# Taking the two heads on the two partition halves together in the mixer's attention, their products issued alternately

## The chip, the cores and the metric

The kernel runs on one core of one Trainium2 chip. The metric is the time of one execution on the device in microseconds (us). Three runs of the kernel before took 1867.41 to 1868.89 us, median 1867.45.

## What is computed

Two residual blocks over 512 positions of width 1024, all in float32: a Conformer-like block (SwiGLU feed-forward, a mixer, SwiGLU feed-forward) and a block with an mLSTM and an RG-LRU layer. The change lies in the mixer, between its input projection and its output projection. Cut to that, the reference is:

```python
u = rms_norm(h, mix_norm)
qa, ka, va, qb, kb, vb, ga, gb = jnp.split(u @ w_in, SPLITS, axis=-1)
ya = neighbourhood_attention_2d(qa, ka, va, na_rpb)   # 8 heads of 64, 8 rows x 16 columns around a query
yb = windowed_gqa_sink(rope(qb), rope(kb), vb, sink)  # 8 query heads of 64 on 2 kv heads, |i-j| <= 128
merged = sigmoid(ga) * (ya @ w_branch_a) + sigmoid(gb) * (yb @ w_branch_b)
h = h + merged @ w_out
```

Both attentions are a score product, a softmax and a value product. In the first a bias is added to the scores; in the second a sink logit joins the denominator.

## The kernel before, in words

**Layout.** Activations lie with features on the 128 partitions and the 512 positions along the free axis. A head is 64 wide, so a tile of queries or keys holds two heads: one on partitions 0 to 63, one on 64 to 127. All projections are one function, `group` (L143): per 128 rows of input three matmuls of 512 columns (`mm3`, L111 to L114; float32 is cut in a high and a low part). A projection with eight input tiles takes 24 such matmuls, and so do the two groups of a `branch` (L310). The attention's own products take float32 operands directly; each such matmul shows in the trace as two passes, each with a weight load, while a transpose shows as one.

**Neighbourhood attention** runs over 16 iterations (L462): tile i (four of them), half hf of the query blocks (two), head e (two).
- `na_scores` (L332) contracts over the 64 partitions of one head: for hf = 0 two matmuls of 256 columns (L343), for hf = 1 one of these and two with 64x64 weights (L346, L347) that go to partitions 0 to 63 and 64 to 127 of the same PSUM tile. `softmax` (L318) adds the bias and takes the row extreme on VectorE (L320), then the exponential and its sum on ScalarE (L322); VectorE scales by the reciprocal (L357, L360).
- `na_values` (L363) transposes the probabilities in pieces of 128 columns on TensorE (L368), copies them to SBUF on ScalarE (L370), and multiplies 64 columns of values by them (L376, L379, L380). The output goes to the head's 64 partitions of the accumulator `po`.

**Windowed attention** runs over 8 iterations (L474): query block nb (four), key-value head g (two).
- `gqa_scores` (L396) makes four matmuls on the 64 partitions of head g (L405), 256 columns wide for nb = 0 and 3, 384 for nb = 1 and 2, each with its softmax, then the scaling (L411 to L416).
- `gqa_values` (L419) goes over two or three key blocks: four transposes (L426), one copy of 512 columns (L428), one product of 512 columns (L429) into half of `po`. `gqa_out` (L432) writes the result (L438, L439) to `yb`.

**Order of the work.** Both loops are pipelined by hand: the scores of the next iteration stand ahead of the values of this one, and in between stands `fills` (L457), which takes projections from a list of 26 (four for later q and k tiles, six for the second attention's inputs, eight gates, the four branches of the first attention, four more gates). In the first loop one fill stands in each iteration, in the second one or two. Behind the loops follow four gates (L486) and the branches of the second attention. The tile framework then orders the instructions of each engine: the earliest in the program goes first if its inputs and its output tile are there, otherwise a later one passes it. The trace shows this order as it came out.

**Tiles.** PSUM has two pools of four banks: `bank` (projections) and `cbank` (scores, transposes, `po`). The pool `chain` (L54) has 18 SBUF tiles: biases, mask, probabilities, the shifted scores `sx`, the transposed copies, and the eight tiles `ya` of the first attention's result, which the four branches of the fill list read.

Of the kernel before, what the change touches and what calls it, by code (L numbers as in the profile page):

```python
# [14 lines left out]
P = 128  # L15
# [7 lines left out]
BIG = 3e38  # L23
# [19 lines left out]
def kernel(ctx: ExitStack, tc: tile.TileContext, a, out):  # L43
# [184 lines left out]
    def mixer(x):  # L228
# [103 lines left out]
        def na_scores(i, hf, e):  # L332
            bias_tile(i)
            if hf:
                bias_tile(4 + i // 2)
            ro = slice(64 * e, 64 * e + 64)
            wid = (256, 256) if hf == 0 else (256, 128)
            ps = cbank()
            for j in range(2):
                b = 2 * hf + j  # L340
                pj = ps[:, 256 * j : 256 * j + wid[j]]
                if b < 3:
                    PE.matmul(pj, qc[i][ro, 64 + 128 * b : 192 + 128 * b], kc[i][ro, 128 * b : 128 * b + 256],  # L343
                              start=True, stop=True)
                else:
                    PE.matmul(pj[0:64], qc[i][ro, 0:64], kc[i][ro, 0:128], start=True, stop=True)  # L346
                    PE.matmul(pj[64:128], qc[i][ro, 448:512], kc[i][ro, 384:512], start=True, stop=True)  # L347
            nm, sm, rc = small(2), small(2), small(2)
            pm = ctile()
            for j in range(2):  # L350
                if 2 * hf + j < 3:
                    bt = bias[i][:, e * 256 : e * 256 + 256]
                else:
                    bt = bias[4 + i // 2][:, (2 * (i % 2) + e) * 128 : (2 * (i % 2) + e) * 128 + 128]
                c = slice(256 * j, 256 * j + wid[j])
                softmax(ps[:, c], wid[j], pm[:, c], bt, nm, sm, j, BIG)
            V.reciprocal(rc, sm)  # L357
            for j in range(2):
                c = slice(256 * j, 256 * j + wid[j])
                V.tensor_scalar(pm[:, c], pm[:, c], rc[:, j : j + 1], None, op0=ALU.mult)  # L360
            return pm, sum(wid)

        def na_values(i, hf, e, po, pm, tot):  # L363
            ro = slice(64 * e, 64 * e + 64)
            hd = slice((2 * i + e) * 64, (2 * i + e) * 64 + 64)
            pt = cbank()
            for c in range(0, tot, P):
                PE.transpose(pt[:, c : c + P], pm[:, c : c + P], ident)  # L368
            ptc = ctile()
            S.copy(ptc[:, :tot], pt[:, :tot])  # L370
            for j in range(2):
                b = 2 * hf + j
                if b < 3:
                    for kb in range(2):
                        c = 256 * j + kb * P
                        PE.matmul(po[ro, 64 + 128 * b : 192 + 128 * b], va[b + kb][:, hd], ptc[:, c : c + P],  # L376
                                  start=kb == 0, stop=kb == 1)
                else:
                    PE.matmul(po[ro, 0:64], va[0][:, hd], ptc[:, 256:320], start=True, stop=True)  # L379
                    PE.matmul(po[ro, 448:512], va[3][:, hd], ptc[:, 320:384], start=True, stop=True)  # L380
# [15 lines left out]
        def gqa_scores(nb, g):  # L396
# [3 lines left out]
            ro = slice(64 * g, 64 * g + 64)  # L400
            nm, sm = small(4), small(4)
            es = []
            for i in range(4):
                ps = cbank()
                PE.matmul(ps[:, :n], bq[i][ro, nb * P : nb * P + P], bk[0][ro, b0 * P : b1 * P], start=True, stop=True)  # L405
                e = ctile()
                softmax(ps[:, :n], n, e[:, :n], mask[0][:, mo : mo + n], nm, sm, i,
                        nsink[0][:, 4 * g + i : 4 * g + i + 1])
                es.append(e)
            rc = small(4)  # L410
            V.tensor_tensor(rc, nm, vc("sink", 4 * g, 4), op=ALU.add)  # L411
            S.activation(rc, rc, AF.Exp)
            V.tensor_tensor(rc, rc, sm, op=ALU.add)
            V.reciprocal(rc, rc)
            for i in range(4):
                V.tensor_scalar(es[i][:, :n], es[i][:, :n], rc[:, i : i + 1], None, op0=ALU.mult)  # L416
            return es

        def gqa_values(nb, g, po, es):  # L419
            b0, b1 = max(0, nb - 1), min(4, nb + 2)  # L420
            ro = slice(64 * g, 64 * g + 64)
            for kb in range(b0, b1):
                pt = cbank()
                for i in range(4):
                    c = (kb - b0) * P
                    PE.transpose(pt[:, i * P : (i + 1) * P], es[i][:, c : c + P], ident)  # L426
                ptc = ctile()
                S.copy(ptc, pt)  # L428
                PE.matmul(po[ro, :], bv[0][:, kb * P + 64 * g : kb * P + 64 * g + 64], ptc,  # L429
                          start=kb == b0, stop=kb == b1 - 1)  # L430
# [31 lines left out]
        its = [(i, hf, e) for i in range(4) for hf in range(2) for e in range(2)]  # L462
        sc = na_scores(*its[0])
        for n, it in enumerate(its):
            fills()
            nxt = na_scores(*its[n + 1]) if n + 1 < len(its) else None
            if n % 4 == 0:
                po = cbank()
            na_values(*it, po, *sc)
            if n % 4 == 3:  # L470
# [573 lines left out]
```

## Time and profile before

| | |
|---|---|
| median of three runs | 1867.45 us |
| the profiled execution, its own time | 1867.34 us |
| its span in the trace | 1865.6 us |
| mean granted TensorE clock | 0.998 |
| TensorE matmul busy (PE) | 1842.9 us, 99% |
| TensorE weight load busy (PEld) | 1488.2 us, 80% |
| VectorE (DVE) / ScalarE (ACT) / GpSimd (POOL) busy | 1085.9 / 709.4 / 23.9 us |
| the stretches of the two attentions | 422.4 to 555.1 us, 555.1 to 666.0 us |

The span is what the trace covers; 1.7 us of the execution lie outside it. Matmul times in the trace overlap (a matmul starts before the one ahead has ended), so the cost of a matmul is read from the distance of two starts, not from its duration. In the timeline one row can stand for several matmuls; its time is from the first start to the last end.

### The profile page before, as it was taken

Reading aid. Unit: us, or ns where it says so; the run is one execution under the profiler, and the core shown is the slowest. Engines: PE = TensorE matmul, PEld = TensorE weight load, DVE = VectorE, ACT = ScalarE, POOL = GpSimd, SP = SyncE. Lnnn points to the kernel's source line nnn. Section 1 sums busy time; section 2 is a strip of 40 time slices with the busy share of each in tenths; the row PEclk is TensorE's granted clock in tenths of the full one; section 3 lists DMA queues with packets and bytes.
Section 4 is the critical chain, followed back from the end, with each engine's and each line's share of the span. In section 5 each row is a group of like instructions: output and inputs, shape, how many; then the busy total and the mean of one; then the engine's idle time right before and its main releaser. Section 6 shows DMA issues by size and latency. Waiting matters only on the chain.

```text
span 1865.6 us, 21147 instructions
## 1 busy us (share of the span) xinstructions
PE 1842.9 (99%) x8320; PEld 1488.2 (80%) x8320; DVE 1085.9 (58%) x1728; ACT 709.4 (38%) x1050; POOL 23.9 (1%) x53
## 2 busy tenths in 40 slices
PE   8999999999999999999999999999999999999998
PEld 6888888877776678788888888788887888888886
DVE  5634435734645456453543475867467476798785
ACT  4322213423344444231322252433434334446762
POOL 0000000000000000000000000000000000000000
PEclk9999999999999999999999999999999999999999
DMA  5332322322321122232232232223222222323222
GB/s 192 93 102 91 102 95 86 102 96 95 103 73 46 57 80 91 90 102 94 99 101 91 85 108 90 80 74 102 74 91 91 79 91 68 101 88 98 88 68 79
DMA packets 50018, 169.53 MB, mean 91 GB/s; under 512 B 5760, under 2 KB 5888, under 8 KB 49920
## 3 DMA queue, kind: packets, MB, share of 16 engines
q1 hardware_dynamic: 48048, 164.91, 26.9%
q10 hardware_dynamic: 1872, 3.29, 0.5%
q8 instruction: 65, 1.06, 0.2%
q14 instruction: 33, 0.27, 0.0%
HBM read 164.77 MB, written 2.10 MB: 89 GB/s over the span
## 4 chain that ended last, share of the span: by engine, by line
PE 85%; issue 12%; DVE 1%; ACT 1%; POOL 1%; DMA 0%; POOLq 0%; ACTq 0%
PE bank L114 25%; PE bank L112 25%; PE bank L113 25%; PE cbank L429 1%; PE cbank L405 1%; PE cbank L662 1%; PE cbank L112 1%; PE cbank L113 1%; PE cbank L114 1%; PE cbank L343 1%; PE cbank L376 1%; POOL small L178 1%; PE cbank L685 1%; PE cbank L686 1%; PE cbank L426 1%
## 5 line engine op out<-in xcount | busy, mean ns | idle before, releaser
L112 PE MATMUL bank<-act,hi 128*128 128x512 f32 x1944 | 760.4, 392 | 6.8 <-ACT act L138 6.7
L113 PE MATMUL bank<-act,hi 128*128 128x512 f32 x1944 | 760.6, 391 | 1.0 <-DVE act L123 0.5
L114 PE MATMUL bank<-act,lo 128*128 128x512 f32 x1944 | 759.7, 391 | 0.0
L97 ACT CAST hi<-raw 128x1024 fp32r<-128x1024 f32 (+2 forms) x315 | 323.2, 1027 | 837.2 <-PE bank L113 541.6
L99 DVE TENSOR_TENSOR lo<-raw,hi 128x1024 fp32r<-128x1024 f32 (+2 forms) x315 | 375.3, 1192 | 135.7 <-ACT hi L97 135.2
L112 PEld LDWEIGHTS bank<-act,hi 128*128 128x128 f32 x1944 | 365.4, 188 | 86.8 <-ACT act L138 6.7
L113 PEld LDWEIGHTS bank<-act,hi 128*128 128x128 f32 x1944 | 365.5, 188 | 84.0 <-DVE act L123 3.8
L114 PEld LDWEIGHTS bank<-act,lo 128*128 128x128 f32 x1944 | 365.6, 188 | 78.2 <-issue 3.1
L196 DVE TENSOR_TENSOR act<-bank,rb 128x512 f32<-128x512 f32 x70 | 48.3, 690 | 117.5 <-PE bank L114 117.3
L223 DVE SCALAR_TENSOR_TENSOR h<-bank,h 128x512 f32<-128x512 f32 x48 | 33.2, 692 | 112.2 <-PE bank L114 111.9
L112 PE MATMUL bank<-hi,act 128*128 128x512 f32 x224 | 88.5, 395 | 0.0
L114 PE MATMUL bank<-hi,act 128*128 128x512 f32 x224 | 87.9, 393 | 0.0
L216 DVE TENSOR_TENSOR act<-bank,rb 128x512 f32<-128x512 f32 x42 | 29.0, 691 | 101.1 <-PE bank L114 101.1
L113 PE MATMUL bank<-lo,act 128*128 128x512 f32 x224 | 87.8, 392 | 0.0
L121 ACT CAST act<-act 128x512 fp32r<-128x512 f32 x96 | 59.6, 621 | 69.4 <-DVE act L217 28.7
L123 DVE TENSOR_TENSOR act<-act 128x512 fp32r<-128x512 f32 x96 | 65.9, 686 | 12.9 <-ACT act L121 12.2
L785 DVE SCALAR_TENSOR_TENSOR act<-act,vec 128x511 f32<-128x511 f32 (+2 forms) x84 | 62.7, 747 | 1.7
L112 PE MATMUL bank<-chain,hi 128*128 128x512 f32 x160 | 62.6, 392 | 0.0
L113 PE MATMUL bank<-chain,hi 128*128 128x512 f32 x160 | 62.6, 391 | 0.0
L114 PE MATMUL bank<-chain,lo 128*128 128x512 f32 x160 | 62.5, 391 | 0.0
L198 ACT ACTIVATE act<-act 128x512 f32<-128x512 f32 x72 | 45.3, 630 | 31.1 <-DVE act L196 30.7
L200 DVE SCALAR_TENSOR_TENSOR act<-act 128x512 f32<-128x512 f32 x72 | 49.4, 686 | 8.7 <-ACT act L198 8.7
(225 smaller groups left out, 1614.2 us busy)
## 6 DMA issues: line engine op xcount, KB each, us to landing
raw<-in_gu_dram SPq DMA_DIRECT2D x88, 512.0 KB, 3.2
raw<-in_mh_dram SPq DMA_DIRECT2D x64, 512.0 KB, 3.2
raw<-in_win_dram SPq DMA_DIRECT2D x34, 512.0 KB, 3.2
raw<-in_dn_dram SPq DMA_DIRECT2D x32, 512.0 KB, 3.5
raw<-in_mo_dram SPq DMA_DIRECT2D x16, 512.0 KB, 3.2
raw<-in_dn_dram SPq DMA_DIRECT2D x16, 384.0 KB, 3.1
raw<-in_rxr_dram SPq DMA_DIRECT2D x12, 512.0 KB, 3.2
raw<-in_rg_dram SPq DMA_DIRECT2D x12, 512.0 KB, 3.2
```

The source lines that it names most:

```text
L97: S.copy(hi[:, :cols], raw[:, :cols])
L99: V.tensor_tensor(lo[:, :cols], raw[:, :cols], f(hi[:, :cols]), op=ALU.subtract)
L112: PE.matmul(ps, st[0], mv[0], start=start, stop=False)
L113: PE.matmul(ps, st[0], mv[1], start=False, stop=False)
L114: PE.matmul(ps, st[1], mv[0], start=False, stop=stop)
L121: S.copy(hi, x)
L123: V.tensor_tensor(lo, x, f(hi), op=ALU.subtract)
L196: V.tensor_tensor(g, ps, rb, op=ALU.mult)
L198: S.activation(th, g, AF.Tanh, scale=0.5)
L200: V.scalar_tensor_tensor(s, th, 1.0, g, op0=ALU.add, op1=ALU.mult)
L223: V.scalar_tensor_tensor(x[o], ps, 0.25, x[o], op0=ALU.mult, op1=ALU.add)
L785: V.scalar_tensor_tensor(c[:, s:], t[:, : T - s], vc(w, j * nt + i), c[:, s:], op0=ALU.mult, op1=ALU.add)
```

## The change

In both attentions one iteration now handles both heads of a tile. The first loop has 8 iterations (i, hf), the second 4 (nb).
- Scores: two `cbank` tiles, one for each head; the matmuls of the heads alternate.
- Values: both heads are transposed and copied first (the second head's transposes go to a tile of the pool `bank`), then the value products alternate, head by head, into the two halves of `po`.
- Fills: in the first loop one before and one after the next scores; in the second one within the scores, after the second pair, one before and one after them (none within or ahead of those of nb = 0 but the one within). The list itself and the pools stay as they are.

The softmax, scaling and output lines are the same instructions for each head, in the order first head, second head.

```diff
@@ na_scores
+            pss = [cbank() for _ in range(2)]
+            ros = [slice(64 * e, 64 * e + 64) for e in range(2)]
             for j in range(2):
                 b = 2 * hf + j
+                for e, ro in enumerate(ros):
+                    pj = pss[e][:, 256 * j : 256 * j + wid[j]]
+                    if b < 3:
+                        PE.matmul(pj, qc[i][ro, 64 + 128 * b : 192 + 128 * b], kc[i][ro, 128 * b : 128 * b + 256],
+                                  start=True, stop=True)
+                    else:
+                        PE.matmul(pj[0:64], qc[i][ro, 0:64], kc[i][ro, 0:128], start=True, stop=True)
+                        PE.matmul(pj[64:128], qc[i][ro, 448:512], kc[i][ro, 384:512], start=True, stop=True)
...
@@ na_values
+            for e, pm in enumerate(pms):
+                pt = (cbank, bank)[e]()
...
+                S.copy(ptc[:, :tot], pt[:, :tot])
+                ptcs.append(ptc)
             for j in range(2):
                 b = 2 * hf + j
+                for kb in range(2):
+                    for e, ptc in enumerate(ptcs):
...
+                            PE.matmul(po[ro, 64 + 128 * b : 192 + 128 * b], va[b + kb][:, hd], ptc[:, c : c + P],
+                                      start=kb == 0, stop=kb == 1)
...
@@ gqa_scores
             for i in range(4):
+                pss = [cbank() for _ in range(2)]
+                for ps, ro in zip(pss, ros):
+                    PE.matmul(ps[:, :n], bq[i][ro, nb * P : nb * P + P], bk[0][ro, b0 * P : b1 * P],
+                              start=True, stop=True)
...
+                if i == 1:
+                    fills(1)
...
@@ gqa_values
             for kb in range(b0, b1):
+                ptcs = []
+                for g in range(2):
+                    pt = (cbank, bank)[g]()
...
+                    S.copy(ptc, pt)
+                    ptcs.append(ptc)
+                for g, ptc in enumerate(ptcs):
+                    PE.matmul(po[64 * g : 64 * g + 64, :], bv[0][:, kb * P + 64 * g : kb * P + 64 * g + 64], ptc,
+                              start=kb == b0, stop=kb == b1 - 1)
...
@@ the loops
-        its = [(i, hf, e) for i in range(4) for hf in range(2) for e in range(2)]
+        its = [(i, hf) for i in range(4) for hf in range(2)]
...
             fills()
             nxt = na_scores(*its[n + 1]) if n + 1 < len(its) else None
+            fills()
...
+        sc = gqa_scores(0, fills)
+        for nb in range(4):
+            fills()
+            nxt = gqa_scores(nb + 1, fills) if nb < 3 else None
+            fills()
+            po = cbank()
+            gqa_values(nb, po, sc)
+            gqa_out(nb, po)
             sc = nxt
```

## Rows read from the trace of the kernel before

**Rows 1.** The page, part 1: busy time of the engines and share of the span.

```profile
PE 1842.9 (99%) x8320; PEld 1488.2 (80%) x8320; DVE 1085.9 (58%) x1728; ACT 709.4 (38%) x1050; POOL 23.9 (1%) x53
```

**Rows 2.** Busy time by stretch: time, then each engine, granted clock, DMA share, GB/s.

```profile
422.40:555.10 132.70, 132.70 (x658) 98.34 (x657) 67.35 (x163) 47.97 (x108) 0.96 (x3) 1.00 0.27 88
555.10:666.00 110.90, 110.82 (x445) 69.89 (x443) 56.54 (x157) 49.12 (x121) 0.00 (x0) 1.00 0.16 53
```

**Rows 3.** Timeline of TensorE, one score block between projections: start, time, what, count.

```profile
428.63 0.39 PE L113 MATMUL bank<-act,hi 128*128 128x512 f32 x1
428.85 0.39 PE L114 MATMUL bank<-act,lo 128*128 128x512 f32 x1
429.17 1.13 PE L343 MATMUL cbank<-act 64*128 64x256 f32 x4
430.23 0.66 PE L368 MATMUL cbank<-ident,chain 128*128 128x128 f32 x4
430.64 0.48 PE L112 MATMUL bank<-act,hi 128*128 128x512 f32 x1
430.96 0.39 PE L113 MATMUL bank<-act,hi 128*128 128x512 f32 x1
```

**Rows 4.** Timeline, a score block with the 64x64 products, weight loads (PEld) too.

```profile
437.53 0.70 PE L343 MATMUL cbank<-act 64*128 64x256 f32 x2
...
438.16 0.32 PE L346 MATMUL cbank<-act 64*64 64x128 f32 x1
...
438.16 0.32 PE L347 MATMUL cbank<-act 64*64 64x128 f32 x1
...
438.21 0.13 PEld L346 LDWEIGHTS cbank<-act 64*64 64x64 f32 x1
...
438.32 0.27 PE L347 MATMUL cbank<-act 64*64 64x128 f32 x1
...
438.52 0.66 PE L368 MATMUL cbank<-ident,chain 128*128 128x128 f32 x4
```

**Rows 5.** Groups by line, 422.3 to 666: busy us, mean ns of one.

```profile
L343 PE MATMUL cbank<-act 64*128 64x256 f32 x48 | 14.6, 411 | 0.0
L376 PE MATMUL cbank<-chain,v 128*64 128x128 f32 x96 | 13.9, 281 | 0.0
L405 PE MATMUL cbank<-act 64*128 64x384 f32 x32 | 11.4, 495 | 0.0
L405 PE MATMUL cbank<-act 64*128 64x256 f32 x32 | 8.5, 396 | 0.0
L343 PEld LDWEIGHTS cbank<-act 64*128 64x128 f32 x48 | 7.7, 185 | 6.1 <-PE bank L113 3.9 <-issue 1.4 <-DVE act L280 0.4
```

**Rows 6.** Timeline of TensorE, windowed attention: two blocks of scores.

```profile
590.23 2.84 PE L405 MATMUL cbank<-act 64*128 64x384 f32 x8
...
640.64 1.99 PE L405 MATMUL cbank<-act 64*128 64x256 f32 x8
```

**Rows 7.** Timeline of TensorE, first attention: a block of value products.

```profile
440.96 1.09 PE L376 MATMUL cbank<-chain,v 128*64 128x128 f32 x8
```

**Rows 8.** Timeline, windowed attention: three copies (ACT) and the value products behind them.

```profile
614.00 1.52 ACT L428 COPY chain<-cbank 128x512 f32<-128x512 f32 x3
...
614.90 1.07 PE L429 MATMUL cbank<-chain,act 128*64 128x512 f32 x2
615.90 0.50 PE L114 MATMUL bank<-act,lo 128*128 128x512 f32 x1
616.24 0.40 PE L112 MATMUL bank<-act,hi 128*128 128x512 f32 x1
616.57 1.07 PE L429 MATMUL cbank<-chain,act 128*64 128x512 f32 x2
```

**Rows 9.** Groups by line, 555 to 666: the softmax of the windowed attention, ScalarE and VectorE.

```profile
L322 ACT ACTIVATE chain<-chain,small 128x384 f32<-128x384 f32 x16 | 9.8, 612 | 6.1 <-DVE small L320 6.1
L320 DVE CUSTOM_DVE_ANT_0 chain<-cbank,chain,nsink 128x384 f32<-128x384 f32 x16 | 9.4, 617 | 0.7 <-PE cbank L405 0.5 <-ACT chain L322 0.2
```

More of the change, by code (lines that the diff above doesn't have):

```diff
@@ L348, in na_scores @@
[L348 to L360, printed above, removed]
@@ new lines, in na_scores @@
+            pms = []
+            for e, ps in enumerate(pss):
+                nm, sm, rc = small(2), small(2), small(2)
+                pm = ctile()
+                for j in range(2):
+                    if 2 * hf + j < 3:
+                        bt = bias[i][:, e * 256 : e * 256 + 256]
+                    else:
+                        bt = bias[4 + i // 2][:, (2 * (i % 2) + e) * 128 : (2 * (i % 2) + e) * 128 + 128]
+                    c = slice(256 * j, 256 * j + wid[j])
+                    softmax(ps[:, c], wid[j], pm[:, c], bt, nm, sm, j, BIG)
+                V.reciprocal(rc, sm)
+                for j in range(2):
+                    c = slice(256 * j, 256 * j + wid[j])
+                    V.tensor_scalar(pm[:, c], pm[:, c], rc[:, j : j + 1], None, op0=ALU.mult)
+                pms.append(pm)
@@ L394, in gqa_consts, with gqa_scores @@
             nsink.append(t)
-        def gqa_scores(nb, g):
+        def gqa_scores(nb, fills):
             b0, b1 = max(0, nb - 1), min(4, nb + 2)
@@ L399, in gqa_scores @@
             mo = (b0 - nb + 1) * P
-            ro = slice(64 * g, 64 * g + 64)
-            nm, sm = small(4), small(4)
-            es = []
+            ros = [slice(64 * g, 64 * g + 64) for g in range(2)]
+            nms, sms = ([small(4) for _ in range(2)] for _ in range(2))
+            es = ([], [])
             for i in range(4):
[L404 to L409, printed above, removed]
@@ new lines, in gqa_scores @@
+                for g, ps in enumerate(pss):
+                    e = ctile()
+                    softmax(ps[:, :n], n, e[:, :n], mask[0][:, mo : mo + n], nms[g], sms[g], i,
+                            nsink[0][:, 4 * g + i : 4 * g + i + 1])
+                    es[g].append(e)
+                if i == 1:
+                    fills(1)
+            for g in range(2):
+                rc = small(4)
+                V.tensor_tensor(rc, nms[g], vc("sink", 4 * g, 4), op=ALU.add)
+                S.activation(rc, rc, AF.Exp)
+                V.tensor_tensor(rc, rc, sms[g], op=ALU.add)
+                V.reciprocal(rc, rc)
+                for i in range(4):
+                    V.tensor_scalar(es[g][i][:, :n], es[g][i][:, :n], rc[:, i : i + 1], None, op0=ALU.mult)
@@ L417, in gqa_scores, with gqa_values @@
             return es
-        def gqa_values(nb, g, po, es):
+        def gqa_values(nb, po, es):
             b0, b1 = max(0, nb - 1), min(4, nb + 2)
-            ro = slice(64 * g, 64 * g + 64)
             for kb in range(b0, b1):
[L423 to L430, printed above, removed]
+                ptcs = []
+                for g in range(2):
+                    pt = (cbank, bank)[g]()
+                    for i in range(4):
+                        c = (kb - b0) * P
+                        PE.transpose(pt[:, i * P : (i + 1) * P], es[g][i][:, c : c + P], ident)
+                    ptc = ctile()
+                    S.copy(ptc, pt)
[3 more added lines that the diff above has]
+                              start=kb == b0, stop=kb == b1 - 1)
```

62 lines of the change are left out of this document (16 added, 46 removed).

## The prediction, made before the changed kernel was run

> **What bounds the kernel now.** I read the page first: TensorE is busy for 99% of the span, the next engine for 58% [rows 1]. A gain must therefore be TensorE time; time taken from VectorE or ScalarE buys nothing unless TensorE waits for it. Then the windows of the two attentions: 132.7 and 110.9 us, TensorE busy throughout at a granted clock of 1.00, which is its 2.4 GHz level, while VectorE has 67 and 57 us of work and ScalarE 48 and 49 [rows 2]. So TensorE bounds both stretches, and about half of the other engines' time is free.
>
> Next the timeline of TensorE, for what a block of attention products costs there. Projections start 0.22 us apart. The last one before a score block is followed after 0.32, and the first one behind the transposes is followed after 0.32 as well [rows 3]: going into a block with narrower weights and coming back costs about 0.10 each way, 0.2 a block. The score block itself, two matmuls in four passes on one half of the partitions, holds TensorE for 1.06 us (429.17 to 430.23) [rows 3]. With the mean duration of one pass, 0.411 [rows 5], the distance of two passes is (1.13 - 0.41) / 3 = 0.24 us; the rest of the 1.06 is the tail until other weights follow. In the windowed attention a pass takes (2.84 - 0.495) / 7 = 0.335 us at 384 columns and (1.99 - 0.396) / 7 = 0.228 at 256 [rows 5, 6].
>
> The row that decides is one where two products use different parts of the array. L346 and L347 have 64x64 weights on the same partitions and write to the two partition halves of one PSUM tile. Their first passes start together at 438.16, their second ones at 438.32 [rows 4]: four passes, two at a time. Side by side is thus possible here, for float32 operands with two passes each. A pair of passes took 0.16 us; one pass of the same 128 columns alone takes (1.09 - 0.281) / 7 = 0.116 [rows 5, 7]. The pair was 1.38 times as long as one, where one behind the other would be 2 times.
>
> **The change part by part.** The sum is made against the profiled execution, 1867.34 us; the median of the runs is 0.1 above it, so nothing is corrected.
>
> *Scores of the first attention.* Before, each of 8 (tile, half) pairs has two blocks; after, one. All inputs are there, the two PSUM tiles are free, and so the order should keep the heads alternating. The heads lie on different halves of the partitions and write to different banks. A pair-step lies between 1.0 and 1.38 times a single step if they overlap. The 0.16 us of the pair in the trace are above its 0.13 us weight load [rows 4], so there the load seems to set the pace; here the load takes 0.185 and the step is already 0.24 [rows 5]. I take 1.0. Then a block for both heads takes what one head's took, and per tile one block of 1.06 [rows 3] and one of 438.52 - 437.53 = 0.99 [rows 4] go away: 4 x 2.05 = **-8.2 us**. Bounds: at 1.38, 8 blocks x 3 steps x 0.24 x 0.38 = 2.2 of this comes back; if the second head's 64x64 pair runs behind the first's, 4 x 0.32 = 1.3. Eight ways in are saved, but the transposes, which followed the scores directly, now come behind a fill, so eight ways out are added: 0.
>
> *Scores of the windowed attention.* Before, 8 blocks of 8 passes; after, the same passes in 4-step blocks for two pairs of matmuls, two of them to a query block. Two of the four query blocks have 384 columns: 16 passes x 0.335 = 5.4 saved; the two with 256: 16 x 0.228 = 3.6. **-9.0 us**, 3.4 less at 1.38. If only two PSUM tiles are free at a time, each pair stands alone: 8 blocks more, 8 x 0.2 = 1.6 back.
>
> A rule of the Trainium skill, page "TensorE: Matmul & The Clock Gate", section on packing small matmuls, gives a measured factor of 3.07 for four row tiles in place of four. An estimate from it, 3.07 / 4 = 0.77 of ideal, would make a pair-step 1.30 times a single one; the paired steps (24 x 0.24 + 16 x 0.335 + 16 x 0.228 = 14.8 us) would grow by 4.4 and the forecast would be 1855.5. The pair in the trace, at 1.38, agrees that two need not cost one.
>
> *Value products.* Here the order matters. Each head's product needs its own copy from PSUM, and ScalarE makes the copies one by one: three took 1.52, so 0.51 us apart [rows 8]. In the windowed attention today the products behind such copies do not stand together in the order: product at 614.90, two projection matmuls, product at 616.57 [rows 8]. The order puts projections wherever the next product is not ready when its turn comes. After the change the two heads' copies are again 0.51 apart, so the second head's product is late by as much, and in the first attention all products of the first head (8 passes, about 1 us [rows 7], fewer in the planner's eyes if two projections fit between) can go before the second's begin. I take no overlap: first attention **0**, windowed **0**. Bounds below are the rival B. Above: a first product split off its block adds one block for each of 8 iterations, the way in and out 0.2 and about 0.1 of tail, 2.4 in all.
>
> *Softmax, scaling, copies, output, fills.* Same instructions, same list of 26 fills; the cover is the projection stream, 24 x 0.22 = 5.3 us to a fill, against about 1.2 us for one softmax on both engines [rows 9]. The second head's transposes take a bank from the projections' pool: a group holds one of the four for 5.3 us, so one is to spare: 0. No DMA is added or moved past another; the fills keep their order, so the weight loads do too. If the cover goes, that is rival D.
>
> Sum: -8.2 - 9.0 = -17.2; I leave 1 us for products that stand together today and may be parted: 1867.3 - 16.2 = **1851 us**. Its own range: up with 2.2 + 3.4 + 1.3 + 1.6 + 2.4 = 10.9 to 1862; down by 4, if a fifth of the value products happen to meet, to 1847.
>
> **Rivals.**
> B, the value products pair as well. For: they are issued alternately, the two halves of `po` are different columns of the array just as in [rows 4], and the order may have no projection ready between. Against: [rows 8]. Price: first attention, 4 blocks of 1.09 [rows 7] and 4 of about 0.85 (half of their products have 64 columns; an estimate from that row) plus 8 x 0.2 = 9.4; windowed, ten products of 1.0 (614.90 to 615.90 [rows 8]) and ten changes of 0.2 = 12. Together -21: **1830**.
> The same page of the Trainium skill says that a weight load runs beside matmuls only where the row groups differ; the two heads' value products share all rows. By that, 84 paired passes x 0.13 us of load would come on top, 10.9, and B would give 1841. Rows 4 speak against it: a load of L346 started at 438.21, while passes on the same rows that began at 438.16 and last 0.32 were running.
>
> C, the two halves do not overlap in the array: the passes of a matmul keep the other head's from starting, or two banks at once don't work. For: the trace has no case of two 64-row products. Against: [rows 4]. Only the tails of eight blocks fall away, (1.06 - 4 x 0.24) x 8 = 0.8: **1867**. This is also the case in which the change doesn't do what it says.
>
> D, slower: the pool `chain`, 18 tiles. Today the windowed attention needs 8 (`ya`) + 1 (mask) + 4 + 4 (probabilities of two iterations) + 1 (`sx`) = 18. After the change it is 8 for each query block: with `ya` there, the second block finds no room until the last of the four branches has run, and later 8 + 8 + 1 + 1 leave one tile for the copies in turn with `sx`. If the planner spends the gates in the meantime, nothing covers the chain that is left: 24 softmaxes of 0.617 + 0.612 = 1.23 us [rows 9], 29.5 us, and 20 steps of transposes 0.41 [rows 3], copy 0.51, way to the product 0.39 (614.51 to 614.90) and product 1.0 [rows 8], 46 us; of these 75, 28 are TensorE's own. That exposes 48 us less 5.3 for each gate left to run. It eats the whole gain when fewer than six of the eight gates are left once `ya` is free; with three left it costs 32: 1851 + 32 = **1883**. Against: VectorE and ScalarE are half idle, the branches themselves are work, and the chain need not be fully serial.
>
> **How the numbers follow.** Forecast A 0.50, B 0.20, C 0.14, D 0.12, mixed outcomes between A and C 0.04. What a measurement can tell from no change is about 0.2%, 3.7 us. Faster by more: A, B and the mixed ones, 0.74; within: C, 0.14; slower: D, 0.12. The range takes in A, C and the upper half of B: 1830 to 1868, leaving out D and half of B, 0.2 in all. A alone would be 1847 to 1862.
>
> **What would show it.** Right: a score block of both heads in about 1.06 us with the heads' passes starting in pairs, a windowed one of four steps in about 1.4 us, two to a query block; value products of the two heads apart with projections between; the first stretch shorter by about 8 us, the second by about 9, all else unchanged. B: value products starting in pairs. C: the passes of the two heads 0.24 apart, not together. D: gaps on TensorE between 590 and 660 us that end on a copy (L428's successor) or a softmax. The forecast is wrong if the time is above 1862 or if the value products give as much as the scores.

## The result, and the profile after

| | before | after |
|---|---|---|
| median of the runs taken together | 1867.43 us | 1849.21 us |
| lowest to highest | 1865.71 to 1868.89 | 1846.18 to 1849.27 |
| profiled execution / its span | 1867.34 / 1865.6 | 1849.27 / 1847.2 |

The ratio is 0.9898, with an interval of 0.9886 to 0.9910: 18.2 us faster, where 16.2 had been forecast. Later the same kernel was measured once more: 1846.06 us (1843.97 to 1847.16), ratio 0.9880 (0.9865 to 0.9895). The kernel before took 1868.71 beside it. Two measurements of one program thus stand 3 us apart, which limits what the medians below can say of small edits; those are read from their traces. The last section shows where the 3 us lie.

In the changed kernel the scores of the first attention are L344, L347 and L348 (before L343, L346, L347), its transposes L372 (L368), copies L374 (L370) and value products L384, L387, L389 (L376, L379, L380). In the windowed attention the scores are L415 (L405), the transposes L442 (L426), the copies L444 (L428), the value products L447 (L429).

The page's first part, after:

```profile
PE 1822.0 (99%) x8320; PEld 1478.5 (80%) x8320; DVE 1083.3 (59%) x1728; ACT 709.8 (38%) x1050; POOL 23.9 (1%) x53
```

Against [rows 1], TensorE has as many instructions and 20.9 us less busy time, and its share is 99% again. The other engines hardly changed. The gain is TensorE time, as forecast.

Busy time by stretch, after, in the columns of [rows 2]:

```profile
422.30:544.90 122.60, 120.27 (x657) 90.83 (x657) 66.02 (x163) 48.55 (x108) 1.01 (x3) 0.99 0.30 95
544.90:641.70 96.80, 96.47 (x427) 62.69 (x423) 55.04 (x157) 48.68 (x121) 0.00 (x0) 1.00 0.18 61
```

The first stretch has one matmul record less than in [rows 2] and is 10.1 us shorter. The second is 14.1 shorter with 18 matmuls less; projections follow each other in 0.23 us, so 18 x 0.23 = 4.1 of it only moved out of the stretch and 10.0 are won. Both attentions gave about 10 us. In the first, TensorE now stands idle for 2.3 us (122.60 - 120.27), which it did not before.

By kind of block, counted from a block's first start to the first start of what follows, summed over all blocks of the profiled execution in us. The ways are what the step from a projection to a block, and the step behind the first projection after one, take above the 0.22 us from projection to projection:

| block | before | after | measured | forecast |
|---|---|---|---|---|
| scores, first attention | 16.4 | 8.3 | -8.1 | -8.2 |
| scores, windowed | 19.2 | 13.8 | -5.3 | -9.0 |
| value products, first | 14.6 | 10.7 | -3.9 | 0 |
| value products, windowed | 19.3 | 16.0 | -3.3 | 0, +1 for parted ones |
| transposes, first | 5.8 | 8.4 | +2.6 | 0 |
| transposes, windowed | 8.2 | 10.5 | +2.2 | 0 |
| ways in and out of the projections | 13.2 | 9.7 | -3.5 | 0 |

This gives -19.3. The attentions' own time, all of this with the smaller kinds, fell from about 97 to 77.5 us; the level shifts by about 1 us with the step that is taken for a projection, 0.22 or 0.23, the difference by less than half. All else took about 1768.5 us before and 1769.7 after. So the sum was close partly by luck: the value products (7.2) and the ways (3.5) gave 10.7 us that were not expected, while the windowed scores stayed 3.7 short and the transposes took 4.8, 8.5 together.

**The score blocks.** Timeline of TensorE, after: the first block with hf = 0, and one with the 64x64 products.

```profile
421.97 0.39 PE L114 MATMUL bank<-hi,act 128*128 128x512 f32 x1
422.29 1.13 PE L344 MATMUL cbank<-act 64*128 64x256 f32 x8
423.36 0.50 PE L112 MATMUL bank<-act,hi 128*128 128x512 f32 x1
...
429.02 0.70 PE L344 MATMUL cbank<-act 64*128 64x256 f32 x4
429.65 0.32 PE L347 MATMUL cbank<-act 64*64 64x128 f32 x1
429.66 0.32 PE L348 MATMUL cbank<-act 64*64 64x128 f32 x1
429.66 0.32 PE L347 MATMUL cbank<-act 64*64 64x128 f32 x1
429.67 0.32 PE L348 MATMUL cbank<-act 64*64 64x128 f32 x1
...
430.03 0.50 PE L112 MATMUL bank<-act,hi 128*128 128x512 f32 x1
```

Eight passes take 1.07 us (422.29 to 423.36), where four took 1.06 in [rows 3]. A pair costs what one costs, as the prediction took it; the bound of 1.38 from [rows 4] did not come. That bound was a misreading: it held the step from first to second pass, 0.16 us, against the mean step of a block. In the block of [rows 7], one head alone, the trace's records of single passes also have the first two 0.16 apart, and the others 0.11. In the second block four products start within 0.02 us and the block takes 1.01, where one head alone took 0.99 [rows 4]. The mean of a pass is still 411 ns [rows 5].

**The value products.** Timeline of TensorE in the first attention, after:

```profile
437.21 0.43 PE L384 MATMUL cbank<-chain,v 128*64 128x128 f32 x2
437.57 0.50 PE L114 MATMUL bank<-act,lo 128*128 128x512 f32 x1
437.90 0.40 PE L112 MATMUL bank<-act,hi 128*128 128x512 f32 x1
438.23 1.09 PE L384 MATMUL cbank<-chain,v 128*64 128x128 f32 x14
439.25 0.50 PE L113 MATMUL bank<-act,hi 128*128 128x512 f32 x1
```

The same of ScalarE, the weight loads and TensorE in the windowed attention:

```profile
588.18 0.56 ACT L444 COPY chain<-cbank 128x512 f32<-128x512 f32 x1
588.64 0.58 ACT L444 COPY chain<-bank 128x512 f32<-128x512 f32 x1
588.92 1.42 PE L447 MATMUL cbank<-chain,act 128*64 128x512 f32 x4
...
589.27 0.19 PEld L447 LDWEIGHTS cbank<-chain,act 128*64 128x64 f32 x2 [0.16 <-ACT chain L444]
...
590.28 0.33 PE L442 MATMUL cbank<-ident,chain 128*128 128x128 f32 x1
```

The second head's copy does come about half a microsecond late, as forecast: 588.64 against 588.18. But in the first attention only the first product goes alone (two passes, 0.36 us) before two projections; the other 14 passes then stand together and take 1.02 us (438.23 to 439.25). Before, eight passes of one head took that long [rows 7]. In the other seven iterations the first product goes alone as well. In this block of the windowed attention no projection goes between: the second head's weights are loaded at 589.27, 0.35 after the first product began, and both are done after 1.36 us (588.92 to 590.28), where one product took 1.0 [rows 8]. It is one of the better ones. Of the ten pairs of windowed products one took 1.01 us, two 1.35 to 1.39 and five 1.49 to 1.75; the last two came as single products of 1.0.

**The windowed scores.** Timeline of TensorE, after, three of its blocks for nb = 1 (the first two) and 2, and a weight load within the third:

```profile
565.54 0.91 PE L415 MATMUL cbank<-act 64*128 64x384 f32 x2
...
573.64 0.91 PE L415 MATMUL cbank<-act 64*128 64x384 f32 x2
...
593.10 3.90 PE L415 MATMUL cbank<-act 64*128 64x384 f32 x12
...
594.73 0.29 PEld L415 LDWEIGHTS cbank<-act 64*128 64x128 f32 x2 [0.69 <-DVE small L320]
```

A wait of ScalarE in the same stretch, in the timeline:

```profile
584.27 0.62 ACT L322 ACTIVATE chain<-chain,small 128x384 f32<-128x384 f32 x1 [2.35 <-PE bank L113]
```

The block of 12 passes is six pair-steps, 2.1 us by [rows 6], and took 3.83 (593.10 to 596.93). The first two lines are two passes each, one head alone. ScalarE's wait, 2.35 us for a projection's matmul rather than for a score, is the pool `chain` as rival D described it: the second query block's probabilities wait until the last branch has read `ya`. Projections covered this wait, so it cost no gap; it cost pairs.

This is only part of the loss. Held against full blocks of four steps (1.49 us at 384 columns, 1.06 at 256), the second query block lost 1.0 us. The third lost 1.7, after the last branch's matmuls had ended (586.5): there no projection stands between these scores, and from the third step on heads come singly, waiting for VectorE's softmax to free a PSUM tile (0.69 us in the line above, then 0.53 and 0.24). The first query block lost 0.9 in two blocks of one head each (543.68 and 546.94).

**A new wait.** Timeline of TensorE, first attention, after:

```profile
494.51 0.60 PE L372 MATMUL cbank<-ident,chain 128*128 128x128 f32 x4
497.24 0.66 PE L297 MATMUL bank<-ident,act 128*128 128x128 f32 x4 [2.13 <-DVE act L294]
```

Busy time and granted clock of that stretch, in the columns of [rows 2]:

```profile
495.00:502.00 7.00, 4.87 (x29) 3.21 (x27) 4.12 (x7) 2.18 (x4) 0.00 (x0) 0.76 0.36 123
```

L297, the transposes of `vb_group`, stands in the order between the two heads' transposes and waits 2.13 us for VectorE (L294). VectorE finishes a piece of the second head's softmax there (L363, until 495.0), then works on two products of a rotation (L278 and L279, to 496.1) before it comes to L294. The granted clock then averaged 0.76 over 7 us. That is about half of the stretch at the lower level, 1.2 GHz, an estimate from the two levels. The prediction had set this cost at 0.

### The profile page after: what moved, and what is told of

Read it like the earlier page. It is cut to its first block, busy times and chain, and to the rows that moved or that the text cites. A ratio compares the mean times of both kernels' runs of the same rounds, so it can differ in the third digit from the quotient of the medians.

```text
span 1847.2 us, 21163 instructions
## 1 busy us (share of the span) xinstructions
PE 1822.0 (99%) x8320; PEld 1478.5 (80%) x8320; DVE 1083.3 (59%) x1728; ACT 709.8 (38%) x1050; POOL 23.9 (1%) x53
## 3 DMA queue, kind: packets, MB, share of 16 engines
q8 instruction: 65, 1.06, 0.2%
## 4 chain that ended last, share of the span: by engine, by line
PE 83%; issue 13%; DVE 2%; ACT 1%; POOL 1%; DMA 0%; SPq 0%; POOLq 0%; ACTq 0%; DVEq 0%
PE bank L112 25%; PE bank L114 25%; PE bank L113 25%; PE cbank L679 1%; PE cbank L447 1%; PE cbank L112 1%; PE cbank L113 1%; PE cbank L114 1%; PE cbank L415 1%; POOL small L178 1%; PE cbank L702 1%; PE cbank L703 1%; PE cbank L704 1%; PE cbank L384 0%; ACT hi L97 0%
```

## The experiments

The theory after the result had three parts. Side by side in the array needs only that the two halves' matmuls stand next to each other in the order, not that they alternate. The value products pair wherever the copies let them. And what is still missing is lost to three waits: the second head's copy, the pool `chain` and `vb_group`. The rivals were that the alternation itself does it, that the value products don't pair and gain only through other places of the fills, and that the pool costs nothing.

### Value products of the first attention head after head

```diff
-            for j in range(2):
-                b = 2 * hf + j
-                for kb in range(2):
-                    for e, ptc in enumerate(ptcs):
...
+            for e, ptc in enumerate(ptcs):
...
+                for j in range(2):
+                    b = 2 * hf + j
+                    for kb in range(2):
```

> The changed kernel, but in the first attention the value products stand head by head in the program: all of head 0, then all of head 1. In TensorE's order the eight (or six) products of an iteration then stand together, four and four; in the changed kernel the first one stands alone, then projections, then the others alternating. Theory 'alternation': passes start strictly in the order issued, so only neighbours of different heads overlap; a block of 16 passes then takes about 15 x 0.117 + 0.2 = 1.95 us where the changed kernel takes 0.36 + 0.2 + 1.02 = 1.6, and the time goes up by about 2.5 us, to 1851.5. Rival 'own queue for each half': two products of different heads overlap whenever they stand within the same stretch of the order; a block takes about 1.02 us, the parted first product is gone, and the time goes down by about 8 x 0.55 = 4.4 us, to 1845.

Measured: 1847.24 us, ratio 0.9890 (0.9875 to 0.9904). Timeline of TensorE:

```profile
437.16 1.58 PE L384 MATMUL cbank<-chain,v 128*64 128x128 f32 x16
438.67 0.50 PE L114 MATMUL bank<-act,lo 128*128 128x512 f32 x1
```

All 16 passes stand together and take 1.51 us, where one behind the other would be two blocks of 1.02 [rows 7]. The second head's first pass began 0.49 us after the block's start, when its copy had landed, and ran among passes of the first head; from there both heads' passes each go on in steps of 0.11 us. So the overlap does not need the alternation. In six of the eight iterations all products stand in one block like this; in the other two the heads stand apart. In sum the value products take 12.8 us instead of 10.7, and the ways 1.6 less, since the lone first product with its two changes is gone. The median lies between the two that were expected, and between the two measurements of the changed kernel.

### Scores head after head

```diff
-            for j in range(2):
-                b = 2 * hf + j
-                for e, ro in enumerate(ros):
+            for e, ro in enumerate(ros):
+                for j in range(2):
+                    b = 2 * hf + j
...
+                    for g, ro in enumerate(ros):
+                        for k in range(2):
+                            PE.matmul(both[k][g][:, :n], bq[i + k][ro, nb * P : nb * P + P], bk[0][ro, b0 * P : b1 * P],
+                                      start=True, stop=True)
```

> The changed kernel, but the scores stand head by head: in the first attention both matmuls of head 0, then both of head 1; in the windowed attention two of g = 0, then two of g = 1, into the same four PSUM tiles. Theory 'alternation': of four double passes only the middle two are neighbours of different heads, so a block of 1.06 us becomes about 1.8 in the first attention for hf = 0 and the windowed blocks lose three quarters of their overlap: about 4 x 0.75 + 4 x 0.4 + 5 = 10 us more, 1859. Rival 'own queue for each half': the blocks stay at 1.06 us with the heads' passes starting in pairs, and the time stays within 2 us of 1849.

Measured: 1851.84 us, ratio 0.9911 (0.9897 to 0.9926). Timeline of TensorE, a block with hf = 0 and one with hf = 1:

```profile
422.41 1.14 PE L344 MATMUL cbank<-act 64*128 64x256 f32 x8
423.48 0.50 PE L112 MATMUL bank<-act,hi 128*128 128x512 f32 x1
...
429.14 0.70 PE L344 MATMUL cbank<-act 64*128 64x256 f32 x2
429.77 0.32 PE L347 MATMUL cbank<-act 64*64 64x128 f32 x1
...
430.14 0.70 PE L344 MATMUL cbank<-act 64*128 64x256 f32 x2
430.76 0.32 PE L347 MATMUL cbank<-act 64*64 64x128 f32 x1
...
431.13 0.50 PE L112 MATMUL bank<-act,hi 128*128 128x512 f32 x1
```

With hf = 0 the block takes 1.07 us in either order: head after head pairs fully. With hf = 1 it falls apart into two blocks, 1.99 us instead of 1.01, four times: 3.9 us. There the matmuls of the first head change from 64x128 weights to 64x64 ones before the second head's 64x128 come, and the second head begins only 0.99 us after the first (430.14 after 429.14), behind its 64x64 products. The Trainium skill, page "TensorEngine Tiling (Array Packing)", section "Key Properties", says that changing the tiling mode drains TensorE; the trace agrees. In the alternated order the shape changes once for both heads. The windowed scores rose too, from 13.8 to 15.7 us in 15 blocks instead of 12: a full block of four steps takes 1.50, as when alternated, but where only two matmuls come at a time, both are of one head. So what the alternation brings is this: it keeps equal shapes together, and it makes two matmuls that come alone a pair.

### The copies of the second head on VectorE

```diff
-                S.copy(ptc[:, :tot], pt[:, :tot])
+                (S.copy, V.tensor_copy)[e](ptc[:, :tot], pt[:, :tot])
...
-                    S.copy(ptc, pt)
+                    (S.copy, V.tensor_copy)[g](ptc, pt)
```

> The changed kernel, with the copy of the second head's transposes on VectorE instead of ScalarE, in both attentions, so that the two copies can run side by side. Theory: the second head's product is late only because the copies stand one behind the other on ScalarE (about 0.5 us apart); with both ready together the first product no longer stands alone (8 x 0.55 = 4.4 us) and the windowed products pair fully (10 x about 0.4 = 4 us): 1841 to 1845. Rival: VectorE's own queue (projection results come first there) makes this copy as late as before or later: 1848 to 1852.

Measured: 1844.60 us, ratio 0.9876 (0.9859 to 0.9892). Timeline of both copies and of TensorE behind them:

```profile
449.83 0.56 DVE L374 COPY chain<-bank 128x384 f32<-128x384 f32 x1
449.90 0.47 ACT L374 COPY chain<-cbank 128x384 f32<-128x384 f32 x1
450.42 0.67 PE L384 MATMUL cbank<-chain,v 128*64 128x128 f32 x8
450.91 0.30 PE L387 MATMUL cbank<-chain,v 128*64 128x64 f32 x4
451.02 0.30 PE L389 MATMUL cbank<-chain,v 128*64 128x64 f32 x4
451.25 0.50 PE L112 MATMUL bank<-act,hi 128*128 128x512 f32 x1
```

Here the copies end 0.02 us apart and all products of both heads stand in one block of 0.83 us. This happened in three of the eight iterations; in the others the second copy was still behind other work and the first product went alone. The attentions' own time is 74.1 us against 77.5 (76.0 in the second measurement), in the right direction, while the medians, from different sessions, can't confirm a difference of that size.

### The projection of v for the windowed attention earlier in the fills

```diff
-        fill += [kb_group] + [lambda i=i: qb_group(i) for i in range(4)] + [vb_group]
+        fill += [vb_group, kb_group] + [lambda i=i: qb_group(i) for i in range(4)]
```

> The changed kernel, with the projection of the windowed attention's values moved from last to first in its part of the fill list (ahead of the rotated keys and queries). Theory: in the changed kernel TensorE stands from 494.9 to 497.2 us, because the four transposes of those values (L297) stand in its order ahead of attention work and wait for VectorE, which is still busy with the rotations; behind the wait the granted clock is lower for some us. Moved ahead of the rotations the wait goes, 2.4 us and about 1.5 of low clock: 1845 to 1846. Rival: the wait is only moved with the transposes, or another one takes its place: 1848 to 1850.

Measured: 1845.44 us, ratio 0.9878 (0.9863 to 0.9893). Busy time and granted clock of the same stretch:

```profile
495.00:502.00 7.00, 6.95 (x44) 5.10 (x43) 4.82 (x9) 2.05 (x4) 0.00 (x0) 1.00 0.48 145
```

What is left of the wait, in the timeline of TensorE where `vb_group` now runs:

```profile
459.74 0.66 PE L297 MATMUL bank<-ident,act 128*128 128x128 f32 x4 [0.54 <-DVE act L294]
```

TensorE is busy throughout at a clock of 1.00, and the wait shrank from 2.13 to 0.54 us. The attentions' own time is 74.6 us, 2.9 below the changed kernel's profiled execution and 1.4 below its second one (76.0), in which the clock did not fall. The wait was caused by the place in the list.

### One part of the change alone

The first of these kernels keeps the scores of both heads together and goes back to values one head at a time; the second does the reverse. The fills stand between the heads of the part that was taken back.

```diff
@@ scores alone
             for e, pm in enumerate(pms):
...
+                pt = cbank()
...
+                if e == 0:
+                    fills()
@@ values alone
+            for e, ro in enumerate(ros):
+                if e:
+                    fills()
+                pss.append(cbank())
```

> The scores alone: both heads' scores together as in the changed kernel, but the values head by head as before (transposes, copy, products of head 0, a fill, then head 1, all in the pool cbank). Theory: the score blocks fall to half as in the changed kernel (first attention 16.5 to 8.4 us of TensorE, windowed 19.2 to 13.8, about -13.5), the value products stay at the 14.7 and 19.3 us of before: 1867.4 - 13.5 = 1854, between 1852 and 1857. Rival 'the gain is in the number of blocks and the waiting, not in the overlap': the parts do not add, and this one gives back most of it: 1860 or more.

> The values alone: both heads' value products alternating as in the changed kernel, but the scores head by head with a fill between. Theory: the value products fall as in the changed kernel (14.7 to 10.7 and 19.3 to 16.0 us) and fewer blocks lie between projections (about 2 us), the scores stay at 16.5 and 19.2; less about 5 us of waits of transposes on TensorE that the changed kernel showed: 1867.4 - 4 to -9, 1859 to 1864. Rival 'value products do not pair, as forecast': 1866 to 1869.

Measured on one chip, where the kernel before took 1867.17: scores alone 1854.83 us, ratio 0.9936 (0.9921 to 0.9951); values alone 1859.53 us, ratio 0.9960 (0.9946 to 0.9975). Groups by line of TensorE in the attentions, scores alone:

```profile
L443 PE MATMUL cbank<-chain,act 128*64 128x512 f32 x40 | 20.1, 615 | 0.5 <-ACT chain L442 0.2
L344 PE MATMUL cbank<-act 64*128 64x256 f32 x48 | 7.6, 415 | 0.0
```

Values alone, and the same value products (L429) in the kernel before:

```profile
L449 PE MATMUL cbank<-chain,act 128*64 128x512 f32 x40 | 16.4, 618 | 0.3
L347 PE MATMUL cbank<-act 64*128 64x256 f32 x48 | 14.6, 411 | 0.0
...
L429 PE MATMUL cbank<-chain,act 128*64 128x512 f32 x40 | 20.4, 615 | 0.1
```

Each part gives its own gain and leaves the other's busy time near that of before (value products 20.1 and 20.4, scores 14.6 and 14.6 [rows 5]). -12.3 and -7.6 add to -19.9, between the two measurements of the whole change (-18.2 and -22.7). That the value products bring nothing is refuted: the kernel with their part alone has more than a third of the gain. That they gain only through other places of the fills is refuted as well: with the fills moved and the products one head at a time they keep their time of before.

### The pool `chain`

Two edits aimed at the windowed scores. The first puts the windowed copies into another pool of SBUF tiles:

```diff
-                    ptc = ctile()
+                    ptc = vp.tile([P, T + 32], F32, tag="v", name="v")[:, :T]
```

> The changed kernel, with the windowed attention's transposed copies in another pool of SBUF tiles (the five tiles that held the first attention's values and are free by then) instead of the pool chain. Theory: in the changed kernel the windowed stretch loses time because the pool chain is full (the copies take turns for one tile, second block's softmax waits for the last branch); with room for the copies the products stand closer and pair better: 2 to 5 us less, 1844 to 1847. Rival: the projections cover this anyway, or ScalarE's row of copies is the limit: 1848 to 1850.

Measured: 1852.12 us, ratio 0.9920 (0.9905 to 0.9935), slower than the changed kernel by 3 to 6 us. The scores L415 came in 17 blocks instead of 12 and cost 15.5 us instead of 13.8. The windowed value products rose as well, from 16.0 to 17.1 us. The gain that was expected from room for the copies did not come. Why the order became worse was not settled.

The second lets the four branches run before the second block's scores, so that `ya` is free by then. The four gates that stood behind the loops join the list, so that eight gates are left behind the branches instead of four:

```diff
-            fills()
+            fills(5 if nb == 0 else 1)
...
-        fill += [lambda o=o: add_gate(gb, 26 + o) for o in range(4)]
+        fill += [lambda o=o: add_gate(gb, 26 + o) for o in range(KD)]
```

> The changed kernel with another place for the fills of the windowed attention: five (last gate, the four branches) stand ahead of the second query block's scores, and the last four gates join the list. Theory: the windowed scores gained less than forecast because the second block's scores were issued while the eight tiles ya were still held, so that its softmax found no room in the pool chain, the PSUM tiles stayed taken and heads came singly (12 blocks of 64 passes, 13.8 us). With the branches ahead there are 8 blocks of 4 steps, about 10 us on TensorE, and 2 to 4 us less in all: 1845 to 1847. Rival: what the scores gain the value products lose, since nothing else covers their copies: 1848 to 1851.

Measured: 1847.53 us, ratio 0.9894 (0.9877 to 0.9910); the unedited changed kernel, in the same session, 1846.06. Timeline of a score block:

```profile
602.69 1.56 PE L415 MATMUL cbank<-act 64*128 64x384 f32 x8
```

Groups by line of TensorE in the attentions:

```profile
L447 PE MATMUL cbank<-chain,act 128*64 128x512 f32 x40 | 17.5, 618 | 1.5 <-ACT chain L444 1.2
L415 PE MATMUL cbank<-act 64*128 64x384 f32 x32 | 6.2, 509 | 0.0
```

The second line in the changed kernel:

```profile
L415 PE MATMUL cbank<-act 64*128 64x384 f32 x32 | 9.0, 525 | 0.1
```

The 384-column scores, busy for 9.0 us in the changed kernel, now take 6.2 in 1.56 us blocks of four pair-steps, and ScalarE's wait for a branch is gone. That brings back what the second and third query block had lost, 2.7 of the 3.7 us that were missing from the forecast -9.0; the first block's 0.9 stays, and the last block now loses about 1. So the order of the fills parted these heads. That the pool alone did is not shown: the edit also puts 20 or more projections between the score blocks, where the third query block had none, and in the third kernel of the next section ScalarE waits 4.07 us for a branch while its blocks still have four steps. Yet the time did not fall, much as the rival had it: the value products rose from 16.0 to 17.2 us and their transposes from 10.5 to 12.3, both from start to start, with 1.2 us of waits for the copies. It fits that the fills that were spent early are not there later to cover the copies; no run isolates it.

### The edits together, and the changed kernel again

Three kernels combine edits. One has the VectorE copies and the early `vb_group`. One adds the other pool for the copies and writes the shifted scores into the tile of the probabilities (`sx = e`). One has the VectorE copies, the early `vb_group` and the branches first, with `fills(4)` in place of 5. The fourth is the changed kernel without an edit.

> The changed kernel with two edits: copies of the second head on VectorE and the values' projection first. Compared with the run of four edits it leaves the two pool edits out. If those cost time, as the other pool for the copies did alone: 1840 to 1842. If they brought some: 1843 to 1845.

> The changed kernel with four edits: second head's copy on VectorE, the windowed copies in the other pool, the shifted scores written into the tile of the probabilities (one tile of the pool chain less for each softmax), and the values' projection first in its part of the fill list. If the effects add, -4 (copies) -4 (order) -2 to -5 (pools): 1837 to 1841. Rival: they remove the same waits, and the best single one is all there is: 1844.

> The changed kernel with the copies of the second head on VectorE, the values' projection first in the list, four fills ahead of the second block's scores, and the last four gates in the list. If the effects add (-4, -3, -3): 1838 to 1841. Rival: no better than the run with four edits, 1842 to 1845.

> The changed kernel once more, unedited, on the same chip as the three that follow, so that they can be compared with it: 1846 to 1850.

Measured: copies and order 1844.89 us, ratio 0.9874 (0.9859 to 0.9889); with the other pool and `sx = e` 1842.56, 0.9870 (0.9855 to 0.9885); with the branches first **1841.89** (1840.29 to 1842.10), 0.9857 (0.9842 to 0.9872); the changed kernel again 1846.06. The third and the fourth ran on the same chip: 4.2 us apart, the slowest run of the one below the fastest of the other, while the intervals of their ratios still overlap a little (0.9865 to 0.9872). The third has the lowest median of this study. Its groups by line, TensorE:

```profile
L447 PE MATMUL cbank<-chain,act 128*64 128x512 f32 x40 | 16.5, 616 | 0.9 <-DVE chain L444 0.5
...
L415 PE MATMUL cbank<-act 64*128 64x384 f32 x32 | 6.2, 508 | 0.0
```

It keeps the gain of the scores (6.2) without the loss in the value products (16.5, not 17.5), which fits two engines that share the copies. The attentions' own time is 72.4 us, against 76.0 in the changed kernel's profiled execution of that session. That copies and order gained only 1.2 us in the median over the changed kernel, less than their own traces suggest one by one, is below what the medians resolve; in its profiled execution the attentions take about 2 us less than in the changed kernel's of that session.

## Why the prediction was right, and where it was not

**The sign and the place were right.** TensorE bounded both stretches, and time taken from it came out of the total nearly one for one: 19.3 us less in the attentions, 18.1 in the profiled executions.

**First scores, -8.2: right**, measured -8.1. A pair-step costs 1.0 times a single one; the prediction's upper bound of 1.38 came from a misread row, as said above. The Trainium skill, page "TensorE: Matmul & The Clock Gate", section on packing small matmuls, gives 3.07 for four row tiles; by the estimate from it, 1.30 a step, 1.7 us of this term would have come back (24 x 0.24 x 0.30). No run here shows four row tiles; with two, the trace shows nothing lost.

**Windowed scores, -9.0: mis-sized**, measured -5.3. The step that failed is that the order keeps 4-step blocks for pairs of heads. In the second query block, while the branches held `ya`, heads came singly (1.0 us); in the third they came at the pace of VectorE's softmax, with no projection between (1.7); in the first query block one head came alone twice (0.9, not traced). The pool behind the first of these had been written down in rival D, but only as the price of a whole gap; its smaller form, matmuls that come alone, was missing. The prediction's own fallback, 1.6 us for pairs that stand alone, did not hold it either: what was lost were the pairs themselves.

**Value products, 0: wrong**, measured -3.9 and -3.3. Its observation was right, the copies come half a microsecond apart. The conclusion was not. In the first attention the delay parts one product of two passes, and the other 14 still stand together. In the windowed one a product lasts longer (1.0 us) than the delay (0.35), so the second can start beside the first; eight of the ten pairs did, one of them wholly. The prediction compared the delay with the place of the next projection and should have compared it with the length of the work that it delays. Rival B, at -21 for these products, took all of them as paired from the start; about a third of that came. By the prediction's own sign, value products that give as much as the scores, it was not wrong: 7.2 us against 13.4.

The rule on the same page of the Trainium skill, that a weight load runs beside matmuls only where the row groups differ, does not fit: the two heads' value products share all rows, and 14 passes, each with its own load, took the 1.02 us of eight.

**Ways in and out, 0: wrong**, measured -3.5. The prediction set eight ways saved against eight added. In the trace the blocks that follow a projection fell from 65 to 44, since one block for two heads now stands where each head had its own.

**Transposes, 0: wrong**, +2.6 and +2.2. The first attention's share is mostly the 2.13 us wait of L297 and the lower clock behind it. The cover named, the projection stream, was there, but L297 stood in TensorE's order ahead of the next projections, which began at 499.17, and TensorE stood still until L294 had ended. The second share was not traced to one wait.

**C** (no overlap, 1867) fell with the first score block. **D** (1883) did not come: TensorE was busy for 96.5 of 96.8 us in the second stretch, with the chain covered. Its smaller form, pairs lost while `ya` is held, came in the second query block.

## What to carry to other kernels

In this kernel two matmuls on different parts of the array cost one where they stood next to each other in the engine's order and both were ready; whether they alternated mattered where the tile shape changed and where only two matmuls came at a time. So first ask what could part them: a copy that serves both, a pool that admits one at a time, a filler that the order slips between. Compare each delay with the length of the work it delays; and move a filler that waits on a shared engine away from the stretch where that engine has more to do.

## What was not expected of the hardware

The same wait can cost a different clock in two executions of one program. Busy time and granted clock of the stretch around L297's wait in the changed kernel's second measurement, to be held against the line with 0.76 above:

```profile
495.00:502.00 7.00, 4.99 (x36) 3.60 (x34) 4.13 (x7) 2.22 (x4) 0.00 (x0) 1.00 0.36 115
```

TensorE stands idle as long (7.00 - 4.99 against 7.00 - 4.87), but here the clock stayed at 1.00, its 2.4 GHz level. The attentions' own time was 76.0 us, 1.5 less than with the clock at 0.76. That is half of the 3 us between the two profiled executions; the other 1.6 us lie outside the attentions (1769.7 and 1768.1). They lie in a second such place: TensorE stands idle for 1.75 us in both executions (until 753.48 and 752.04, waiting for GpSimd, L178), and from 750 to 760 us the granted clock averaged 0.83 in the first and 1.00 in the second. 10 x (1 - 0.83) = 1.7 us is an estimate of its cost.

Four 64x64 products, two heads on two output halves, run at once: their eight passes start in two groups, 0.16 us apart (429.65 and 429.81), exactly as the four passes of one head did [rows 4].

Whether the second head's windowed scores in the projections' PSUM pool would bring the pairs without touching the fills was not tried.
